# A two-layer decoder trunk: norm heads over six tiles, second statistics behind 18 products, a first FFN whose head weights have tiles of their own, and one more unit ahead of two waits of the scan

## The chip, the core and the metric

The kernel runs on one NeuronCore of a Trainium2 chip. The metric is the device time of one execution in microseconds; 0.3% of it is 3.6 us. The engines are PE (TensorE matmul; its weight loads are PEld), DVE (VectorE), ACT (ScalarE), POOL (GpSimd) and SP (SyncE, which here issues most of the DMAs).

## The reference, cut to what matters

The input is x (1 x 512 x 1024, fp32) and a conditioning vector c. There are two layers. Layer 0 mixes tokens with stick-breaking attention (16 heads), layer 1 with a diagonal complex state-space layer and a GLU; each is followed by a gated MLP with a causal convolution of width 3 (inner width 2816).

```python
def rms_norm(x, g):
    y = x * lax.rsqrt(jnp.mean(x * x, axis=-1, keepdims=True) + EPS)
    return y * g

for i in range(DEPTH):                       # DEPTH = 2
    mod = silu(c) @ w_mod[i] + b_mod[i]
    sh1, sc1, g1, sh2, sc2, g2 = jnp.split(mod, 6, axis=-1)
    h = rms_norm(x, norm_mix[i]) * (1 + sc1) + sh1
    y = stick_breaking_attention(h, ...) if i == 0 else s5_ssm(h, ...)
    x = x + g1 * y
    h = rms_norm(x, norm_ffn[i]) * (1 + sc2) + sh2
    x = x + g2 * conv_ffn(h, w_up[i], conv_w[i], conv_b[i], w_down[i])
return rms_norm(x, norm_out) * (1 + sc) + sh

def s5_ssm(h, ...):
    u = h @ w_in                             # then, in 64 groups of 16 channels,
    states = scan(lam_bar * state + b_bar @ u)
    y = real(c_mat @ states) + d_skip * u
    z = gelu(y)
    return (z * sigmoid(z @ w_glu + b_glu)) @ w_o
```

## The kernel before

**Layout and products.** Channels lie on the 128 partitions and the 512 tokens along the free axis, so x is eight tiles x0 to x7 of 128 x 512. Each fp32 matrix product is made of three products of a rounded high part and a rest: `mm3` (L155 on) issues hi by hi (L158), then weight-hi by input-lo (L161), then weight-lo by input-hi (L162). Such a triple over 512 columns is called a unit below. `load_w` (L143 on) brings a weight block of 0.5 MB into the ring `wraw` (three buffers, issued on SP, L150), ACT makes the high part (L152) and DVE the rest (L153), into rings `wH` and `wL` of `NW` = 5 buffers, or into tiles of the caller's own.

**Heads.** Three places have the same form: attention's output projection followed by the first FFN ("FFN0"), the first FFN's down projection followed by the state-space layer ("SSM"), and the SSM's output projection followed by the second FFN ("FFN1"). There `out_proj` (L339 on) finishes the last three tiles of x (x5, x6, x7) first for the left half of the tokens, then for the right (names ca and cb). ACT squares each updated tile (`acc_sq`, L226 and L229), DVE adds the squares into `acc` (L230), and `rstd_stat` (L263 on) sums `acc` over channels with a matmul of 1 column (L251, tile `stat`), takes the root on ACT (L255, tile `nsd`), refines it on DVE and writes a diagonal `dg`; `rstd_bc` (L270 on) broadcasts it with a matmul (L273, tile `rbc`). `sqrt_table` loads ACT's table for the root ahead of it (L241). Then `head_mm` runs: for the left half of the tokens, tile by tile, `norm_tile` writes hH and hL (DVE L291, ACT L298 and L300, DVE L304) and each of four weights is multiplied with it over 256 columns; the statistics and the broadcast of the right half stand among those products. It does so for the first `HEADK` = 5 tiles, then for the right half of the same tiles, and takes the remaining three over all 512 columns.

**The first FFN's first four weights.** Before, FFN0 loads them through the ring when `ffn` starts (`up_w`); FFN1's come by `head_w`, which `out_proj` calls after the weights of its own last three tiles and ahead of `sqrt_table`. `head_w` gives the first two of its four weights tiles of their own on the right side of the SBUF and leaves the other two to the ring. `HEADW` names the norm tiles behind which the next four weights are split.

**The scan.** After the SSM head, dense work (units of `u = h @ w_in`, later of the GLU) is cut into units that PE runs between the steps of the scan; `run(n)` issues n of them. Ahead of the loop stand `run(UPRE)`, step 0's `st_scan` (matmul `pv`, L1109), `run(USTG[0])`, step 1's, and `run(USTG[1])`. In each turn s of the loop, `st_out` issues `py` (L1109) and, on ACT, `yn` (L1178), `st_scan` issues `pv` for s, `run(1)` issues one unit, `st_tr` issues the transposes `pz` (L1183) that wait for `yn`, and `run(100)` the rest. On ACT the scan's states are written by L1165 (tile `st`, four instructions a step), and DVE runs the recurrence between (L1151 to L1160).

**What sets the order.** A scheduler that simulates the engines orders each engine's instructions, save those that are pinned to program order (`pinned`, `keep_in_program_order`), put behind another (`behind_head`, `follow`) or tied by data. Each engine then runs its own list in order.

Of the kernel before, what the change touches and what calls it, by code (L numbers as in the profile page):

```python
# [30 lines left out]
NW = 5  # L31
MIDK = 1
STATK = 0
HEADK = 5
HEADB = (3, 2)
HEADW = (4, 7, 10, 12)
UPRE = 10
NACC = 6
NIDLE = (7, 4, 4)
USTG = (7, 8)  # L40
BGU = 2
PACE = 12.0
NHOLD = 2
# [18 lines left out]
DUP = 's'  # L62
QK = 'kq'
BGA = 5
BGW = 0
ZM = ((1, 0), (1, 1), (3, 0), (3, 1))
OMB = 9
TAUX = 7
# [20 lines left out]
def _trunk(ctx, tc, I, out, tap):  # L89
# [105 lines left out]
    bgq = []  # L195
# [113 lines left out]
    def head_mm(R, h, a, b, hd):  # L309
        pin["head"] = []  # L310
        for cr in HALF + (FULL,):
            for k in range(HEADK) if cr != FULL else range(HEADK, KD):
                if cr.start == 0 and k == 2:
                    rstd_stat(R, HALF[1], True)
                norm_tile(h, k, R["bc"][0], a, b, cr)
                for q, (w, ps) in enumerate(hd):
                    if cr == HALF[0] and (k, q) == HEADB:
                        rstd_bc(R, HALF[1], None, True)
                    mm3(ps[:, cr], wk(w, k), (h[0][k][:, cr], h[1][k][:, cr]), k == 0 and cr.start == 0, k == KD - 1)
# [85 lines left out]
    def ffn(l, R, prep=None, last=None, hook=lambda: None):  # L405
# [4 lines left out]
        with ExitStack() as fc:  # L410
            fp = fc.enter_context(tc.tile_pool(name=f"ffn{l}", bufs=1, reuse_waits="tile"))

            def up_w(i, s):
                return load_w(up_src(l, i, s), name=f"up{l}_{i}_{s}"), bank(name=f"up{l}_{i}_{s}")


            todo = []
            i0 = 0
# [54 lines left out]
            for gi, gn in enumerate(GROUPS):  # L473
# [2 lines left out]
                if gi == 2:  # L476
                    hook()
                if gi == 0:
                    if l:
                        hx, ws = pin["hw"]  # L480
                        hd = [(q, s, ws[2 * q + s], bank(name=f"up{l}_{q}_{s}")) for q in range(2) for s in range(2)]
                    else:
                        hx = None
                        hd = [(q, s) + up_w(q, s) for q in range(2) for s in range(2)]
                    head_mm(R, h, a, b, [q[2:] for q in hd])
                    if hx:
                        hx.close()
                    for q in range(4):
                        with behind_head(pin["head"][HEADW[q]]):
                            split_next(False)  # L490
                    pin["prep"] = [pin["split"]]
                    for q in range(2):
                        gs.append(unit_out(q, q, [hd[2 * q + s][3] for s in range(2)]))
                    i = 2
                    step = prep(fc) if prep else (lambda: None)
# [31 lines left out]
    def attention(acc, late):  # L527
        with ExitStack() as ac:
# [282 lines left out]
            split(6)  # L811
            window(8, wo_units(range(KPRE, 7)))
            split(7)
            acc2 = new_acc()
            R = out_proj(wsrc, list(zip(oh, ol)), mcol(0, 2, 0), acc2, "wo", part=[(w, ps, 7) for w, ps in part], after=lambda: bg(BGW))
            bg(max(0, len([q for q in bgq if q[0] is not None]) - 72 - 8))
        return R


# [248 lines left out]
    def ssm(R):  # L1068
# [3 lines left out]
        with ExitStack() as zc:  # L1072
# [3 lines left out]
            with ExitStack() as sc:  # L1076
# [147 lines left out]
                for s_ in range(2, 10):  # L1224
                    st_out(s_ - 2)
                    if s_ < 8:
                        st_scan(s_)
                        load_out(s_)
                    if s_ + 1 < 8:
                        load_scan(s_ + 1)  # L1230
                    if s_ > 2:
                        if s_ == 3:
                            zh = new_h()
                            gb = [bank(name=f"glu{mt}") for mt in range(NGLU)]
                        glu_units(s_ - 3)
                    run(1)
                    st_tr(s_ - 2)
                    if s_ >= 8:
                        with behind_head([pin["comb"]]):
                            bg(11 - s_, False)  # L1240
                    run(100)
# [214 lines left out]
```

## Time and profile before

| What | Value |
|---|---|
| time before, median of three runs | 1212.62 us (1210.58 to 1214.79) |
| profiled execution, its own time | 1211.41 us |
| its span, first to last instruction | 1209.4 us |
| mean granted TensorE clock | 0.989 |
| PE busy | 1173.0 us, 97% |
| DVE, ACT, POOL busy | 884.2, 563.8, 264.0 us |

The profiled execution lies 1.21 us below the median of the three runs. Of its time, 2.0 us lie outside the span of instructions. In the span the FFN0 head stands at about 255 to 307 us, FFN0 itself to about 640, the SSM head to about 680, the scan to 790, and the FFN1 head at 832 to 868. In the timeline views a row has a start, a duration, the engine, the line and what it wrote and read; the brackets at its end hold the idle time of that engine just before it, and what ended that.

### The profile page before, as it was taken

The page shows a single profiled execution, that of the slowest core. Times are in us where ns is not written, and L with a number is a line of the kernel's source. Part 1 is how long each engine was busy: PE and PEld are TensorE (multiplying, and loading weights), DVE is VectorE, ACT ScalarE, POOL GpSimd, SP SyncE. Part 2 cuts the span into 40 slices and gives each one's busy share as a digit, 9 for nine tenths or more (in the row PEclk, how much of TensorE's full clock was granted, in tenths as well). Part 3 has the DMA queues.
Part 4 walks back from the last instruction along what each step waited for, and adds up shares of the span by engine and source line. Part 5 has one row for each costly group of instructions (what it writes and reads, how often), then busy time and mean ns, then how long its engine had stood idle before and what let it go on. Part 6 is the DMA issues. An engine that isn't in the chain of part 4 may idle for free.

```text
span 1209.4 us, 16352 instructions
## 1 busy us (share of the span) xinstructions
PE 1173.0 (97%) x6182; PEld 962.7 (80%) x6182; DVE 884.2 (73%) x1298; ACT 563.8 (47%) x886; POOL 264.0 (22%) x241
## 2 busy tenths in 40 slices
PE   8999999899999999989999999999999999999997
PEld 6877776588788787868888878789888888888887
DVE  6968888756896399997886679776598457744655
ACT  6756566346553133422444657744554234422443
POOL 1000000000098699989630000000000000000003
PEclk9999999899999999989999999999999999999999
DMA  8875555421234867878665599542257438532221
GB/s 306 319 242 174 192 175 190 157 88 53 73 119 131 239 235 225 252 229 291 217 184 152 188 292 342 186 159 68 70 175 236 130 106 208 157 110 82 79 79 70
DMA packets 93536, 210.99 MB, mean 174 GB/s; under 512 B 19601, under 2 KB 39953, under 8 KB 93458
## 3 DMA queue, kind: packets, MB, share of 16 engines
q1 hardware_dynamic: 85138, 207.86, 54.1%
q10 hardware_dynamic: 8320, 2.10, 0.8%
q8 instruction: 48, 0.79, 0.3%
q14 instruction: 30, 0.25, 0.1%
HBM read 188.68 MB, written 21.24 MB: 174 GB/s over the span
## 4 chain that ended last, share of the span: by engine, by line
PE 66%; DVE 12%; POOL 8%; DMA 6%; ACT 4%; issue 3%; SPq 2%; POOLq 0%; ACTq 0%; DVEq 0%
PE up L161 9%; PE up L162 9%; PE up L158 9%; PE dn L161 5%; PE dn L158 5%; PE dn L162 5%; PE o L756 1%; DMA bt<-in_b_imT_dram 1%; PE wo L158 1%; PE wos L158 1%; DVE ca L443 1%; PE wos L162 1%; PE wos L161 1%; PE wo L162 1%; PE wo L161 1%
## 5 line engine op out<-in xcount | busy, mean ns | idle before, releaser
L162 PE MATMUL up<-hH,up_l 128*128 128x512 f32 (+1 forms) x692 | 265.0, 385 | 4.9 <-DVE up_l L153 4.9
L161 PE MATMUL up<-hL,up_h 128*128 128x512 f32 (+1 forms) x692 | 264.9, 385 | 0.3 <-DVE hL L304 0.2
L158 PE MATMUL up<-hH,up_h 128*128 128x512 f32 (+1 forms) x692 | 261.3, 385 | 1.1 <-ACT hH L298 1.1
L443 DVE SCALAR_TENSOR_TENSOR ca<-up,small,ca 128x511 f32<-128x511 f32 (+1 forms) x176 | 131.4, 747 | 85.4 <-ACT ca L441 82.5
L183 DVE SCALAR_TENSOR_TENSOR wg<-wg,cact 128x1024 f32<-128x1024 f32 x96 | 125.1, 1318 | 42.4 <-DMA wg<-in_w_modT_dram 42.2
L162 PEld LDWEIGHTS up<-hH,up_l 128*128 128x128 f32 x692 | 130.5, 189 | 32.1 <-DVE up_l L153 6.8
L161 PEld LDWEIGHTS up<-hL,up_h 128*128 128x128 f32 x692 | 130.4, 189 | 26.4 <-DVE hL L304 0.9
L158 PEld LDWEIGHTS up<-hH,up_h 128*128 128x128 f32 x692 | 128.3, 188 | 27.9 <-ACT hH L298 1.5
L161 PE MATMUL dn<-gL,dn_h 128*128 128x512 f32 (+1 forms) x394 | 145.5, 369 | 2.7 <-DVE gL L458 2.7
L158 PE MATMUL dn<-gH,dn_h 128*128 128x512 f32 (+1 forms) x394 | 145.7, 371 | 0.5 <-ACT gH L457 0.5
L162 PE MATMUL dn<-gH,dn_l 128*128 128x512 f32 (+1 forms) x394 | 145.3, 369 | 0.0
L152 ACT ACTIVATE up_h<-up_r 128x1024 fp32r<-128x1024 f32 x84 | 88.3, 1053 | 107.6 <-DMA up_r<-in_w_up_dram 54.0
L153 DVE TENSOR_TENSOR up_l<-up_r,up_h 128x1024 fp32r<-128x1024 f32 x84 | 124.5, 1482 | 15.8 <-ACT up_h L152 14.9
L1328 POOL TENSOR_SCALAR xa<-x,Anorm_out 128x256 f32<-128x256 f32 x7 | 5.8, 828 | 576.3 <-ACT dn_h L152 561.5
L441 ACT ACTIVATE ca<-up,small 128x512 f32<-128x512 f32 x88 | 67.8, 771 | 102.4 <-PE up L162 102.4
L161 PEld LDWEIGHTS dn<-gL,dn_h 128*128 128x128 f32 x394 | 74.9, 190 | 15.3 <-DVE gL L458 3.0
L158 PEld LDWEIGHTS dn<-gH,dn_h 128*128 128x128 f32 x394 | 74.8, 190 | 13.7 <-ACT gH L457 0.9
L162 PEld LDWEIGHTS dn<-gH,dn_l 128*128 128x128 f32 x394 | 74.9, 190 | 12.2
L334 DVE SCALAR_TENSOR_TENSOR x<-dn,mod,x 128x512 f32<-128x512 f32 (+1 forms) x55 | 37.3, 679 | 61.1 <-PE dn L162 61.0
L450 ACT ACTIVATE ca<-ca 128x512 f32<-128x512 f32 x44 | 27.8, 633 | 90.1 <-DVE ca L443 88.4
L152 ACT ACTIVATE dn_h<-dn_r 128x1024 fp32r<-128x1024 f32 (+1 forms) x48 | 46.6, 981 | 49.8 <-PE dn L161 36.6
L153 DVE TENSOR_TENSOR dn_l<-dn_r,dn_h 128x1024 fp32r<-128x1024 f32 (+1 forms) x48 | 63.7, 1328 | 3.2 <-ACT dn_h L152 3.0
(304 smaller groups left out, 2258.8 us busy)
## 6 DMA issues: line engine op xcount, KB each, us to landing
wg<-in_w_modT_dram SPq DMA_DIRECT2D x96, 512.0 KB
up_r<-in_w_up_dram SPq DMA_DIRECT2D x84, 512.0 KB
dn_r<-in_w_down_dram SPq DMA_DIRECT2D x32, 512.0 KB
wgs<-in_w_modT_dram SPq DMA_DIRECT2D x16, 512.0 KB
dn_r<-in_w_down_dram SPq DMA_DIRECT2D x16, 384.0 KB
wv_r<-in_w_v_dram SPq DMA_DIRECT2D x8, 512.0 KB
wk_r<-in_w_qk_dram SPq DMA_DIRECT2D x8, 512.0 KB
wq_r<-in_w_qk_dram SPq DMA_DIRECT2D x8, 512.0 KB
```

The source lines that it names most:

```text
L152: order("S", lambda: S.activation(wh[:, :n], raw[:, :n], AF.Copy))
L153: pin["split"] = order("V", lambda: V.tensor_tensor(wl[:, :n], raw[:, :n], wh[:, :n].bitcast(F32), ALU.subtract))
L158: ins = PE.matmul(ps, ah, bh, start=start, stop=False)
L161: PE.matmul(ps, ah, bl, start=False, stop=False)
L162: PE.matmul(ps, al, bh, start=False, stop=stop)
L183: mul = lambda: V.scalar_tensor_tensor(w, w, 1.0, cact, ALU.mult, ALU.mult, accum_out=raw[:, col:col + 1])
L334: add = lambda: V.scalar_tensor_tensor(xs, pv, gate, xs, ALU.mult, ALU.add)
L441: follow("S", lambda: S.activation(ca, ps, AF.Identity, bias=small[:, cb:cb + 1], scale=tapw[2]))
L443: follow("V", lambda: V.scalar_tensor_tensor(ca[:, q:], ps[:, :T - q], tapw[2 - q], ca[:, q:], ALU.mult, ALU.add))
L450: follow("S", lambda: S.activation(cg, cg, AF.Silu))
L756: ins = PE.matmul(po[pr][h2 * HD:(h2 + 1) * HD, j * P:], vn[:, j, hd:hd + HD], src, start=j == 0, stop=j == 3)
L1328: G.tensor_scalar(xa[k], x[k][:, cb], a[:, k:k + 1], 0.0, ALU.mult, ALU.add)
```

## The change

It has four parts. (Behind the first FFN's code the lines of the kernel now are eight lower: L1109 is L1101, L1178 is L1170, L1183 is L1175.) `HEADK` goes from 5 to 6 in all three heads, and the second `rstd_stat` moves in the code from ahead of norm tile 2 (24 matmuls in) to inside tile 1 behind its second weight (18 matmuls in). FFN0's first four weights come by `head_w` under the name `upo`, as FFN1's do, and so are loaded inside attention's `out_proj`, which is now called after attention's own pool is closed; the two remaining calls of `bg` there are dropped (they ran no step, as 58 of at most 80 were left). `HEADW` counts norm tiles and follows `HEADK`, so that its weights are split behind the same tiles as before or one later. In the scan, `UPRE` goes from 10 to 12, `USTG` from (7, 8) to (6, 7), and the loop's `run(1)` becomes `run(2)`.

```diff
--- before.py
+++ after.py
@@ -31,13 +31,14 @@
 NW = 5
 MIDK = 1
 STATK = 0
-HEADK = 5
+HEADK = 6
+HEADS = (1, 2)
 HEADB = (3, 2)
-HEADW = (4, 7, 10, 12)
-UPRE = 10
+HEADW = (4, 8, 11, 13)
+UPRE = 12
 NACC = 6
 NIDLE = (7, 4, 4)
-USTG = (7, 8)
+USTG = (6, 7)
 BGU = 2
 PACE = 12.0
 NHOLD = 2
@@ -62,7 +63,6 @@
 DUP = 's'
 QK = 'kq'
 BGA = 5
-BGW = 0
 ZM = ((1, 0), (1, 1), (3, 0), (3, 1))
 OMB = 9
 TAUX = 7
@@ -310,10 +310,10 @@
         pin["head"] = []
         for cr in HALF + (FULL,):
             for k in range(HEADK) if cr != FULL else range(HEADK, KD):
-                if cr.start == 0 and k == 2:
-                    rstd_stat(R, HALF[1], True)
                 norm_tile(h, k, R["bc"][0], a, b, cr)
                 for q, (w, ps) in enumerate(hd):
+                    if cr == HALF[0] and (k, q) == HEADS:
+                        rstd_stat(R, HALF[1], True)
                     if cr == HALF[0] and (k, q) == HEADB:
                         rstd_bc(R, HALF[1], None, True)
                     mm3(ps[:, cr], wk(w, k), (h[0][k][:, cr], h[1][k][:, cr]), k == 0 and cr.start == 0, k == KD - 1)
@@ -410,9 +410,6 @@
         with ExitStack() as fc:
             fp = fc.enter_context(tc.tile_pool(name=f"ffn{l}", bufs=1, reuse_waits="tile"))
 
-            def up_w(i, s):
-                return load_w(up_src(l, i, s), name=f"up{l}_{i}_{s}"), bank(name=f"up{l}_{i}_{s}")
-
 
             todo = []
             i0 = 0
@@ -476,15 +473,10 @@
                 if gi == 2:
                     hook()
                 if gi == 0:
-                    if l:
-                        hx, ws = pin["hw"]
-                        hd = [(q, s, ws[2 * q + s], bank(name=f"up{l}_{q}_{s}")) for q in range(2) for s in range(2)]
-                    else:
-                        hx = None
-                        hd = [(q, s) + up_w(q, s) for q in range(2) for s in range(2)]
+                    hx, ws = pin["hw"]
+                    hd = [(q, s, ws[2 * q + s], bank(name=f"up{l}_{q}_{s}")) for q in range(2) for s in range(2)]
                     head_mm(R, h, a, b, [q[2:] for q in hd])
-                    if hx:
-                        hx.close()
+                    hx.close()
                     for q in range(4):
                         with behind_head(pin["head"][HEADW[q]]):
                             split_next(False)
@@ -811,9 +803,9 @@
             split(6)
             window(8, wo_units(range(KPRE, 7)))
             split(7)
-            acc2 = new_acc()
-            R = out_proj(wsrc, list(zip(oh, ol)), mcol(0, 2, 0), acc2, "wo", part=[(w, ps, 7) for w, ps in part], after=lambda: bg(BGW))
-            bg(max(0, len([q for q in bgq if q[0] is not None]) - 72 - 8))
+        acc2 = new_acc()
+        R = out_proj(wsrc, list(zip(oh, ol)), mcol(0, 2, 0), acc2, "wo", part=[(w, ps, 7) for w, ps in part],
+                     head=([up_src(0, q, s) for q in range(2) for s in range(2)], "upo"))
         return R
 
 
@@ -1233,7 +1225,7 @@
                             zh = new_h()
                             gb = [bank(name=f"glu{mt}") for mt in range(NGLU)]
                         glu_units(s_ - 3)
-                    run(1)
+                    run(2)
                     st_tr(s_ - 2)
                     if s_ >= 8:
                         with behind_head([pin["comb"]]):
```

**FFN0's head on ACT.** The rows stand behind the split of the last weight of attention's projection, `wo7`; `up0_i_s` and `upo0` to `upo3` are the FFN's first four weights, `sq` is a square of a tile of x (x5 to x7 by halves). Before:

```order
L241 ACT_TABLE_LOAD
L241 ACTIVATE warm_2364<-ones_102 128x1
L229 ACTIVATE sq_2263<-x1_79 128x512
L229 ACTIVATE sq_2270<-x2_80 128x512
L152 ACTIVATE up0_0_0_h_2576<-up0_0_0_r_2575 128x1024
L229 ACTIVATE sq_2305<-x3_81 128x512
L152 ACTIVATE up0_0_1_h_2583<-up0_0_1_r_2582 128x1024
L229 ACTIVATE sq_2340<-x4_82 128x512
L229 ACTIVATE sq_2393<-x5_83 128x256
L229 ACTIVATE sq_2421<-x6_84 128x256
L229 ACTIVATE sq_2449<-x7_85 128x256
L152 ACTIVATE up0_1_0_h_2590<-up0_1_0_r_2589 128x1024
```

And now:

```order
L229 ACTIVATE sq_2264<-x1_79 128x512
L229 ACTIVATE sq_2271<-x2_80 128x512
L152 ACTIVATE upo0_h_2369<-upo0_r_2368 128x1024
L229 ACTIVATE sq_2306<-x3_81 128x512
L152 ACTIVATE upo1_h_2375<-upo1_r_2374 128x1024
L152 ACTIVATE upo2_h_2381<-upo2_r_2380 128x1024
L229 ACTIVATE sq_2341<-x4_82 128x512
L152 ACTIVATE upo3_h_2387<-upo3_r_2386 128x1024
L241 ACT_TABLE_LOAD
L241 ACTIVATE warm_2392<-ones_102 128x1
L229 ACTIVATE sq_2421<-x5_83 128x256
L229 ACTIVATE sq_2449<-x6_84 128x256
```

The table load and its warm-up have moved from ahead of the first square to behind the split of the fourth weight, and the splits of the third and fourth weight from behind the left half's squares of x5 to x7 to ahead of them.

**FFN0's head on PE.** `stat` are the second statistics; around them stand the four weights' products with hH and hL (L158, L161, L162 over 256 columns). Before:

```order
L158 MATMUL up_1_0_2595<-hH_2557,up_1_0_h 128x256
L158 MATMUL up_1_1_2602<-hH_2557,up_1_1_h 128x256
L251 MATMUL stat<-ones,acc 128x1 x2
L161 MATMUL up_0_0_2581<-hL_2565,up_0_0_h 128x256
L162 MATMUL up_0_0_2581<-hH_2557,up_0_0_l 128x256
```

And now:

```order
L158 MATMUL up_1_0_2604<-hH_2584,upo_h 128x256
L158 MATMUL up_1_1_2605<-hH_2584,upo_h 128x256
L251 MATMUL stat<-ones,acc 128x1 x2
L161 MATMUL up_0_0_2602<-hL_2592,upo_h 128x256
L162 MATMUL up_0_0_2602<-hH_2584,upo_l 128x256
```

The second statistics stand in the same place of PE's list as before, behind the high products of the third norm tile; the broadcast that follows 20 products later (tile `rbc`) is in its old place too. It is the same in FFN1's head; in the SSM head the statistics stand four products earlier and the broadcast in its old place.

**The scan on PE, turn 2, step 0's transposes.** `u` is the dense work; `pv` is step 2's, `pz` step 0's. Before:

```order
L1109 MATMUL py_6525<-pC,st_6322 64x128 x8
L1109 MATMUL pv_6545<-u,pB 64x64 x16
L158 MATMUL u_6494<-hH_5992,win_h 128x512
L161 MATMUL u_6494<-hL_6000,win_h 128x512
L162 MATMUL u_6494<-hH_5992,win_l 128x512
L1183 MATMUL pz<-consts,yn 128x128 x4
L158 MATMUL u_6494<-hH_5993,win_h 128x512
L161 MATMUL u_6494<-hL_6001,win_h 128x512
```

And now:

```order
L1101 MATMUL py_6565<-pC,st_6362 64x128 x8
L1101 MATMUL pv_6585<-u,pB 64x64 x16
L158 MATMUL u_6537<-hH_6014,win_h 128x512
L161 MATMUL u_6537<-hL_6022,win_h 128x512
L162 MATMUL u_6537<-hH_6014,win_l 128x512
L158 MATMUL u_6537<-hH_6015,win_h 128x512
L161 MATMUL u_6537<-hL_6023,win_h 128x512
L162 MATMUL u_6537<-hH_6015,win_l 128x512
L1175 MATMUL pz<-consts,yn 128x128 x4
L158 MATMUL u_6537<-hH_6016,win_h 128x512
```

A second unit of three products stands between `pv` and `pz`. It is so in each turn.

**The scan on ACT, the same turn.** `st` are the states of a step, `wglk_h` a split of a GLU weight, `z` reads the transposes. Before:

```order
L1115 ACTIVATE ut<-u_6424 128x512
L1116 DMA sU<-ut 128x8x64
L1165 ACTIVATE st_6323<-m_6478 64x4x63 x4
L152 ACTIVATE wglk_h<-wglk_r 128x640
L1178 ACTIVATE yn<-py_6525 128x4x8x16
L1186 ACT_TABLE_LOAD
L1186 ACTIVATE z_6010<-pz 64x4x64 x4
```

And now:

```order
L1107 ACTIVATE ut<-u_6470 128x512
L1108 DMA sU<-ut 128x8x64
L1170 ACTIVATE yn<-py_6565 128x4x8x16
L1157 ACTIVATE st_6363<-m_6521 64x4x63 x2
L152 ACTIVATE wglk_h<-wglk_r 128x640
L1157 ACTIVATE st_6363<-m_6521 64x4x63 x2
L1178 ACT_TABLE_LOAD
L1178 ACTIVATE z_6032<-pz 64x4x64 x4
```

`yn` of step 0 has moved from behind the four `st` of step 1 and a weight split to ahead of them.

## The prediction

> **What bounds the kernel now.** I read the page's busy times first, then its chain.
>
> ```profile
> PE 1173.0 (97%) x6182; PEld 962.7 (80%) x6182; DVE 884.2 (73%) x1298; ACT 563.8 (47%) x886; POOL 264.0 (22%) x241
> PE 66%; DVE 12%; POOL 8%; DMA 6%; ACT 4%; issue 3%; SPq 2%; POOLq 0%; ACTq 0%; DVEq 0%
> ```
>
> PE works 97% of the span, so the change can win only where PE idles or is throttled. Then I cut the span into stages and asked what PE waited for in each (columns: PE, PEld, DVE, ACT, POOL busy, granted clock, DMA share, GB/s; for a wait: total us, times, longest).
>
> ```profile
> 255.00:286.00 31.00, 28.94 (x222) 27.67 (x221) 24.83 (x52) 19.35 (x32) 0.00 (x0) 1.00 0.40 120
> 305.00:326.00 21.00, 20.88 (x93) 16.95 (x91) 19.28 (x66) 10.54 (x15) 0.00 (x0) 1.00 0.22 75
> 442.00:523.00 81.00, 76.45 (x371) 60.81 (x369) 79.81 (x69) 33.77 (x47) 78.51 (x50) 1.00 0.79 241
> 705.00:790.00 85.00, 82.22 (x750) 67.56 (x748) 70.12 (x118) 61.72 (x118) 0.00 (x0) 1.00 0.80 270
> PE stat L251 <- DVE acc L230: 0.9, 1, 0.9
> PE up L162 <- DVE up_l L153: 4.9, 4, 2.2
> PE dn L161 <- DVE gL L458: 2.7, 1, 2.7
> PE pz L1183 <- ACT yn L1178: 2.8, 4, 1.2
> ```
>
> The FFN0 head (255 to 286) loses 2.1 us and the scan (705 to 790) 2.8. In FFN0 itself PE waits 4.9 for splits and 2.7 for gL, while DVE (79.81 of 81 us) and POOL are full.
>
> **The change part by part.** *Six tiles by halves.* These PE rows (and one of DVE) give the spacing of products and the head's main stall:
>
> ```profile
> 269.70 0.28 PE L161 MATMUL wo<-hL,wo_h 128*128 128x256 f32 x1
> 269.82 0.28 PE L162 MATMUL wo<-hH,wo_l 128*128 128x256 f32 x1
> 271.00 0.61 PE L251 MATMUL stat<-ones,acc 128*128 128x1 f32 x4 [0.91 <-DVE acc L230]
> 283.93 0.59 PE L273 MATMUL rbc<-dg,ones 128*128 128x256 f32 x2
> 285.67 0.74 PE L158 MATMUL up<-hH,up_h 128*128 128x256 f32 x4 [1.15 <-ACT hH L298]
> 325.26 0.39 PE L158 MATMUL up<-hH,up_h 128*128 128x512 f32 x1
> 325.49 0.39 PE L161 MATMUL up<-hL,up_h 128*128 128x512 f32 x1
> 325.49 1.22 DVE L153 TENSOR_TENSOR up_l<-up_r,up_h 128x1024 fp32r<-128x1024 f32 x1
> 326.76 0.50 PE L162 MATMUL up<-hH,up_l 128*128 128x512 f32 x1 [0.89 <-DVE up_l L153]
> ```
>
> A 256-column product takes 0.12 us (269.70 to 269.82), a 512-column one 0.23 (325.26 to 325.49; 0.227 over longer runs). Twelve wide ones become 24 narrow ones in each head: 24 x 0.12 - 12 x 0.227 = +0.16 us, three times +0.47. Behind the second broadcast, PE waits for the first right-half hH (1.15 us). The sixth left tile could cover that only if its products stood behind the broadcast. They do not: statistics and broadcast stand behind the third and fourth tile in the FFN heads as before, and what follows waits for hH of the next tile. I price this part's gain at zero; the cover that would be needed, 12 narrow products, is 1.44 us, which bounds the gain at 1.15 in each head. Moving the SSM's statistics four products up has no wait in the trace to remove: zero.
>
> *FFN0's own weight tiles.* ACT's list in the head, and DVE's last step before the statistics:
>
> ```profile
> 258.50 1.28 ACT L241 ACT_TABLE_LOAD   x1
> 259.79 0.20 ACT L241 ACTIVATE warm<-ones 128x1 f32<-128x1 f32 x1
> 261.44 1.06 ACT L152 ACTIVATE up_h<-up_r 128x1024 fp32r<-128x1024 f32 x1 [0.40 <-DMA up_r<-in_w_up_dram]
> 264.02 1.06 ACT L152 ACTIVATE up_h<-up_r 128x1024 fp32r<-128x1024 f32 x1 [0.72 <-DMA up_r<-in_w_up_dram]
> 268.38 0.95 ACT L229 ACTIVATE sq<-x 128x256 f32<-128x256 f32 x2 [0.92 <-DVE acc L230]
> 270.98 0.40 ACT L229 ACTIVATE sq<-x 128x256 f32<-128x256 f32 x1
> 270.54 0.41 DVE L230 TENSOR_TENSOR acc<-acc,sq 128x256 f32<-128x256 f32 x1
> 264.19 0.33 SPq L150 DMA_DIRECT2D up_r<-in_w_up_dram  x1
> ```
>
> Now the left squares of x5 to x7 stand behind the split of the fourth weight and the table load. The first two weights reached ACT at 261.44 and 264.02, 2.58 apart; the fourth, issued at 264.19 when the ring's first buffer came free, can then be split at about 261.44 + 3 x 2.58 = 269.2. From there: split 1.06, table 1.28, warm 0.20 and three squares (0.95 + 0.40) end at 269.2 + 3.9 = 273.1, one accumulation (0.41) at 273.5, and with 0.15 for hand-overs (my choice) the statistics start at 273.65, against 271.00: +2.65 us. This counts the transfers as one after another. If the fourth took only 2.58 from its issue, it would land at 266.8, and ACT, held by the third split and the square of x4 then, would come some 1.5 us sooner: +1.1, the lower bound.
>
> PE would then stand still from 269.94 to 273.65, 3.7 us. The next rows tell what a stall does to the clock:
>
> ```profile
> 416.82 0.61 PE L162 MATMUL up<-hH,up_l 128*128 128x512 f32 x1 [2.22 <-DVE up_l L153]
> 523.38 0.80 PE L161 MATMUL dn<-gL,dn_h 128*128 128x512 f32 x1 [2.67 <-DVE gL L458]
> 417.10:420.50 3.40, 3.40 (x9) 2.61 (x9) 1.38 (x2) 0.09 (x1) 2.23 (x3) 0.50 1.03 370
> 523.00:529.80 6.80, 6.42 (x28) 4.49 (x29) 6.80 (x7) 1.06 (x1) 4.11 (x3) 0.51 0.89 271
> ```
>
> After the wait of 2.22 the granted clock is 0.50 for 3.4 us, after that of 2.67 for 6.8; at half clock half of that time is lost, so a stall of 3.7 costs a further 1.7 (one window) to 3.4 (two); I take one. [...]
>
> On the other side, two splits (DVE L153, 1.2 us each) that stood behind the head now come inside it. That takes 2.4 us from DVE in the stage 305 to 326, where it is 92% busy and at whose end PE waits 0.89. By spacing that wait costs 326.76 - 325.49 - 0.227 = 1.04; a bracket counts some 0.15 less than is lost, and I add that to the others. This wait goes: -1.04. FFN0 so comes to 327 by 0.16 + 2.65 + 1.7 - 1.04 = 3.47 us late. What later waits return of this depends on whether their releasers come from PE. The largest, at 416.82, does not:
>
> ```profile
> SPq L955 <- POOL tb L835: 16.0, 1, 16.0
> POOL tt L834 <- ACT si L888: 86.4, 1, 86.4
> ```
>
> SP's transfers, the split's among them, were held by a store that waited 16.0 us for POOL, and POOL's work began behind ACT's `si`, whose preparation on DVE stands beside FFN0's own steps and gains the 2.4 us. So if PE comes 3.47 later, the wait there (2.22 + 0.15) and the loss in the throttled window behind it (3.4 x 0.5 = 1.7), together 4.1, can go. A whole return has the 2.4 us for it, none the order of DVE's list; I take three quarters, -3.0. FFN0 in all: +0.47.
>
> *The scan.* Its waits by place:
>
> ```profile
> 698.72 1.15 PE L1109 MATMUL pv<-u,pB 128*64 128x64 f32 x32 [0.84 <-issue]
> 716.54 0.66 PE L1183 MATMUL pz<-consts,yn 128*128 128x128 f32 x4 [1.20 <-ACT yn L1178]
> 746.49 0.66 PE L1183 MATMUL pz<-consts,yn 128*128 128x128 f32 x4 [0.24 <-ACT yn L1178]
> 760.79 0.66 PE L1183 MATMUL pz<-consts,yn 128*128 128x128 f32 x4 [1.10 <-ACT yn L1178]
> 715.27 0.74 ACT L152 ACTIVATE wglk_h<-wglk_r 128x640 fp32r<-128x640 f32 x1
> 715.91 0.58 ACT L1178 ACTIVATE yn<-py 128x512 f32<-128x512 f32 x1
> 726.00:733.00 7.00, 6.76 (x83) 5.51 (x82) 6.62 (x13) 5.08 (x12) 0.00 (x0) 1.00 1.04 368
> ```
>
> A unit is 3 x 0.227 = 0.68 us. The first `pv` waited 0.84 + 0.15 for u's way through DRAM; two units ahead of it, 1.36, cover that: -1.0. The `pz` at 716.54 waited 1.35: a unit takes 0.68, and `yn` now runs ahead of the split at 715.27 (0.74): -1.35. The one at 746.49 waited 0.39, and so did the fourth of the group (2.8 less 1.2, 1.1 and 0.24): -0.8. The last, 1.25, keeps what a unit leaves: -0.68. The sum is -3.8. Between the steps each `pv` needs operands from DRAM, and the DMA share is full (1.04 at 726), so part may come back: I take -3.5, with bounds of -0.5 (transfers hold each step where it was, and half of the first wait's gain is left) and -3.8.
>
> *The rest* (the dropped `bg` calls, the pool's end) issues nothing: zero.
>
> **The sum.** Heads of SSM and FFN1 +0.31, FFN0 +0.47, scan -3.5: -2.7. The profiled execution's 1211.41 becomes 1208.7; it lies 1.21 below the median of the runs, 1212.62, which becomes **1209.9 us**. About 0.3%, 3.6 us, is what a measurement of this kernel can tell from no change; this is less.
>
> **The rivals.** (A, the forecast) as summed: 0.37. A fifth of it goes beyond -3.6: with the scan's whole 3.8 and the whole 4.1 at 416.82 it is -4.1.
>
> (B) The later waits return nothing, because DVE's preparation stands behind FFN0's delayed steps in its list: 3.0 more than A, +0.3: 1212.9. For it speaks that DVE is full from 442 to 523; against it, the 2.4 us it gains. 0.17.
>
> (C, the other side) The statistics' stall throttles the head for three windows: 10.2 us at half clock cost 5.1 instead of 1.7, none of it returns, and the split at 326.76 is late all the same. Then 0.47 + 2.65 + 5.1 - 3.5 = +4.7: 1217.3. It decides once the clock stays at 0.5 for more than two windows of 3.4 us: the granted clock from 274 to 284 would read 0.5, as the head's next wait (285.67) comes before PE is steady. For it speaks that the 2.67 already cost two windows; against it, that the 2.22 cost one. 0.14.
>
> (D) The transfers keep the scan's pace: -0.5 there, +0.3 in all: 1212.9. The share of 1.04 speaks for it; against it, that `pz` waits for ACT in all four cases. 0.06.
>
> (E) The fourth weight lands early, FFN0 loses 1.1 and no window, and the 2.4 us that DVE gains reach the wait at 416.82: 0.16 + 1.1 - 1.04 - 2.4 = -2.2, with the scan and 0.31 -5.4: 1207.2, and 1205.5 if the throttled window goes too. For it: three transfers are under way at once. 0.17.
>
> (F) The change does in the heads what the rows of PE's list deny: the sixth tile's products cover the broadcast, and three waits of 1.15 go beside A, -3.45: 1206.5. 0.06.
>
> (G) ACT stays held behind the moved table load for another 1.28, the load's own length: 1.3 more than A, 1211.2. The row at 259.79 speaks against it. 0.03.
>
> **Chances and range.** Faster by over 0.3%: a fifth of A, E, F: 0.07 + 0.17 + 0.06 = 0.30. Slower: C, 0.14. Within: 0.56. The range reaches from E's lower end, 1205.5, to 1217.3, the time of C; outside lie half of C and the tails of E and F, some 0.12. A's own range, by the bounds of its terms, is 1208.5 to 1212.9.
>
> **What would show it.** In the head the statistics near 273.6 with a wait on `acc` of about 3.5 and a clock of 0.5 behind them; no wait at 326, a shorter one near 417. In the scan no wait of `pz` before the last and none at the first `pv`. The 1.15 behind each second broadcast still there. The forecast is wrong if the statistics stand before 272, if the wait near 417 keeps its 2.2, or if the stage to 790 is not 3 us shorter.

## The result, and the profile after

The changed kernel takes 1216.07 us (median of 20 runs, 1210.98 to 1221.14); the kernel before, over 20 runs beside them, 1211.88 (1207.1 to 1215.73). The ratio is 1.0031 (95% interval 1.0019 to 1.0043): 3.8 us slower, where 2.7 us faster was forecast.

The profiled execution of the changed kernel is a slow one among its runs (1219.35 us, span 1217.2), so its whole is not compared with 1209.4. The two traces are set side by side by stage, from the first narrow product of attention's last three tiles on. Columns: what the stage runs from and to, before, after, difference.

| Stage | before | after | |
|---|---|---|---|
| start to the first narrow `wo` product | 258.4 | 261.3 | +2.9 |
| FFN0's head and FFN0, to the first product of the SSM | 405.8 | 410.0 | +4.2 |
| SSM head and scan, to the first `wos` product | 125.5 | 126.0 | +0.5 |
| SSM's projection | 45.4 | 45.4 | 0.0 |
| FFN1's head and FFN1, to PE's last product | 367.6 | 367.8 | +0.2 |

The first row lies ahead of every changed instruction but the issue of the first weights, 0.6 us before its end. In the 14 kernels profiled here that stretch takes between 258.4 and 265.0 us, also in kernels that have the same instructions there, so it says nothing of the change. The second row scatters as well: two kernels of the experiments that differ from the kernel before only in the scan take 403.3 and 403.2 us there, where it took 405.8. So its +4.2 may be wrong by 2.6.

PE's waits of the changed kernel in FFN0's head, in FFN0 and in the SSM (total us, times, longest):

```profile
PE stat L251 <- DVE acc L230: 4.6, 1, 4.6
PE up L162 <- DVE up_l L153: 5.3, 7, 1.1
PE dn L161 <- DVE gL L455: 2.7, 1, 2.7
PE pv L1101 <- DMA pB<-sB: 3.0, 1, 3.0
PE pz L1175 <- ACT yn L1170: 1.2, 2, 0.7
336.19 0.50 PE L162 MATMUL up<-hH,up_l 128*128 128x512 f32 x1 [0.68 <-DVE up_l L153]
```

The wait at the statistics has grown from 0.9 to 4.6. The split waits in FFN0 sum to 5.3 where they were 4.9, but the longest has fallen from 2.2 to 1.1. The one at 326, which was to go, is still there (the last row, 0.68 instead of 0.89). In the scan the waits for `yn` have fallen from 2.8 to 1.2, as forecast, and the first `pv` no longer waits; in their place stands one wait of 3.0 that was not there before. ACT's list in FFN0's head and the statistics on PE, as forecast in kind:

```profile
264.24 1.06 ACT L152 ACTIVATE upo_h<-upo_r 128x1024 fp32r<-128x1024 f32 x1 [1.80 <-DMA upo_r<-in_w_up_dram]
266.72 1.06 ACT L152 ACTIVATE upo_h<-upo_r 128x1024 fp32r<-128x1024 f32 x1 [0.50 <-DMA upo_r<-in_w_up_dram]
269.63 1.06 ACT L152 ACTIVATE upo_h<-upo_r 128x1024 fp32r<-128x1024 f32 x1 [1.86 <-DMA upo_r<-in_w_up_dram]
273.15 1.06 ACT L152 ACTIVATE upo_h<-upo_r 128x1024 fp32r<-128x1024 f32 x1 [1.94 <-DMA upo_r<-in_w_up_dram]
274.23 1.28 ACT L241 ACT_TABLE_LOAD   x1
275.63 0.70 ACT L229 ACTIVATE sq<-x 128x256 f32<-128x256 f32 x2
277.60 1.01 PE L251 MATMUL stat<-ones,acc 128*128 128x1 f32 x4 [4.59 <-DVE acc L230]
```

ACT waits 1.94 for the fourth weight, splits it, loads the table and only then squares the left halves; the statistics start 4.45 us behind the start of the fourth split. The clock in the stretch behind (columns as in the prediction), beside the SSM's two windows around the new wait:

```profile
272.70:277.60 4.90, 0.31 (x3) 0.11 (x2) 3.20 (x7) 3.99 (x7) 0.00 (x0) 0.92 0.51 159
277.60:283.60 6.00, 6.00 (x28) 6.00 (x29) 1.53 (x8) 0.26 (x1) 0.00 (x0) 0.50 0.13 53
740.00:747.00 7.00, 7.00 (x85) 5.95 (x84) 6.60 (x13) 5.38 (x13) 0.00 (x0) 1.00 0.43 129
747.00:754.00 7.00, 4.05 (x69) 3.33 (x67) 4.03 (x7) 4.74 (x10) 0.00 (x0) 1.00 0.97 330
```

The half clock lasts two windows of 3.4 us, from 276.8, while PE still waits, to 283.6. In the scan the DMA share falls to 0.43 ahead of the wait: it is not that the loads were too slow, they were not issued. SP and ACT's queue there:

```profile
729.30 0.39 ACTq L1108 DMA_DIRECT2D sU<-ut  x1
735.89 1.37 SPq L1082 DMA_DIRECT2D pT<-sT  x1
744.85 0.32 SPq L1083 DMA_DIRECT2D pC<-sC  x1
SPq L1083 <- DMA sU<-ut: 7.5, 1, 7.5
752.96 1.15 PE L1101 MATMUL pv<-u,pB 128*64 128x64 f32 x32 [2.95 <-DMA pB<-sB]
```

SP stands from 737.3 to 744.85 ahead of a load of `pC`, for the landing of the last store of `u`, which ACT issued at 729.30. So that store took 15.5 us; the `pB` behind `pC` in SP's list came too late for `pv`. Why `pC` waits for a store that it does not read stands in the instructions' own waits (order of the changed kernel):

```
ACT  L1108 DMA sU_116<-ut_6658 128x8x64 [waits DMAHW5_49,Activation_49]
SP   L1083 DMA pC_6836<-sC_111 128x1024 [waits DMAHW5_49,PE_49]
```

Both name the semaphore `DMAHW5_49`, and `pC` is the next DMA on it behind the store. Its wait for the landing is the 7.5 us above.

### The profile page after: what moved, and what is told of

It reads as the page before. It is cut to its first block, busy times and chain, and to the rows that moved or that the text cites. A ratio compares the mean times of both kernels' runs of the same rounds, so it can differ in the third digit from the quotient of the medians.

```text
span 1217.2 us, 16434 instructions
## 1 busy us (share of the span) xinstructions
PE 1175.4 (97%) x6218; PEld 966.4 (79%) x6218; DVE 884.6 (73%) x1304; ACT 563.8 (46%) x892; POOL 264.0 (22%) x241
## 4 chain that ended last, share of the span: by engine, by line
PE 72%; DVE 12%; DMA 6%; ACT 4%; issue 3%; POOL 2%; SPq 1%; POOLq 0%; ACTq 0%; DVEq 0%
PE up L158 10%; PE up L161 10%; PE up L162 10%; PE dn L158 6%; PE dn L161 6%; PE dn L162 6%; DVE om L718 2%; DVE up_l L153 2%; DVE ca L440 1%; DMA up_r<-in_w_up_dram 1%; PE wos L158 1%; PE wos L162 1%; PE wos L161 1%; DVE wg L183 1%; PE u L161 1%
## 5 line engine op out<-in xcount | busy, mean ns | idle before, releaser
L162 PE MATMUL up<-hH,up_l 128*128 128x512 f32 x640 | 249.6, 391 | 5.3 <-DVE up_l L153 5.3
L158 PE MATMUL up<-hH,up_h 128*128 128x512 f32 x640 | 250.2, 391 | 0.5 <-ACT hH L298 0.5
L161 PE MATMUL up<-hL,up_h 128*128 128x512 f32 x640 | 249.3, 389 | 0.0
L161 PE MATMUL dn<-gL,dn_h 128*128 128x512 f32 (+1 forms) x394 | 144.8, 368 | 2.7 <-DVE gL L455 2.7
L162 PEld LDWEIGHTS up<-hH,up_l 128*128 128x128 f32 x640 | 120.1, 188 | 33.2 <-DVE up_l L153 8.5
L158 PE MATMUL dn<-gH,dn_h 128*128 128x512 f32 (+1 forms) x394 | 145.4, 370 | 0.0
L162 PE MATMUL dn<-gH,dn_l 128*128 128x512 f32 (+1 forms) x394 | 144.5, 367 | 0.0
L158 PEld LDWEIGHTS up<-hH,up_h 128*128 128x128 f32 x640 | 120.1, 188 | 26.7 <-issue 1.0
L161 PEld LDWEIGHTS up<-hL,up_h 128*128 128x128 f32 x640 | 120.2, 188 | 24.6
L152 ACT ACTIVATE up_h<-up_r 128x1024 fp32r<-128x1024 f32 x80 | 84.1, 1052 | 101.8 <-PE dn L161 37.8
L153 DVE TENSOR_TENSOR up_l<-up_r,up_h 128x1024 fp32r<-128x1024 f32 x80 | 118.3, 1479 | 11.8 <-ACT up_h L152 10.9
L161 PEld LDWEIGHTS dn<-gL,dn_h 128*128 128x128 f32 x394 | 74.6, 189 | 15.1 <-DVE gL L455 3.0
L158 PEld LDWEIGHTS dn<-gH,dn_h 128*128 128x128 f32 x394 | 74.4, 189 | 12.9 <-issue 0.6
L162 PEld LDWEIGHTS dn<-gH,dn_l 128*128 128x128 f32 x394 | 74.6, 189 | 12.3
```

The lines of the kernel that those rows point to most:

```text
L152: order("S", lambda: S.activation(wh[:, :n], raw[:, :n], AF.Copy))
L153: pin["split"] = order("V", lambda: V.tensor_tensor(wl[:, :n], raw[:, :n], wh[:, :n].bitcast(F32), ALU.subtract))
L158: ins = PE.matmul(ps, ah, bh, start=start, stop=False)
L161: PE.matmul(ps, ah, bl, start=False, stop=False)
L162: PE.matmul(ps, al, bh, start=False, stop=stop)
```

## The experiments

All ratios are to the kernel before, run beside them on the same chip, over five rounds.

**Each part alone.** Theory T1 held FFN0's own weight tiles for the loss, T2 the six tiles by halves, T3 the stretch ahead. The first kernel is the kernel before with FFN0's head weights by `head_w`:

```diff
-            R = out_proj(wsrc, ..., after=lambda: bg(BGW))
+        R = out_proj(wsrc, ...,
+                     head=([up_src(0, q, s) for q in range(2) for s in range(2)], "upo"))
```

> The kernel before with one part of the change alone: the first FFN's four head weights by head_w (own tiles, loaded inside attention's out_proj). Theory T1 (the loss of the whole change, +0.31%, is this part: ACT's list in the first FFN's head holds the left squares behind the fourth split and the table load): statistics there wait over 4 us, the granted clock is 0.5 for two windows behind them, the head loses 6 us, later waits give back 2; in all +4 us, ratio 1.0033. Theory T2 (the loss comes from six tiles by halves in all three heads): ratio 1.000, no such wait. Theory T3 (the loss lies in attention, where the changed kernel's trace is 2.9 us later by 212 us, from where tiles lie): +2.9 before 212 us again.

1217.01 us, ratio 1.0050 (1.0032 to 1.0068). T1's wait and clock are there:

```profile
278.39 0.92 PE L250 MATMUL stat<-ones,acc 128*128 128x1 f32 x4 [3.72 <-DVE acc L229]
278.52:285.35 6.83, 6.83 (x32) 6.83 (x33) 1.88 (x9) 0.35 (x2) 0.00 (x0) 0.50 0.10 38
```

The wait is 3.72 and the half clock lasts 6.83 us. By the medians this part alone loses more than the whole change, but the intervals (1.0032 to 1.0068 and 1.0019 to 1.0043) overlap.

The scan's counts alone:

```diff
-UPRE = 10
+UPRE = 12
-USTG = (7, 8)
+USTG = (6, 7)
-                    run(1)
+                    run(2)
```

> The kernel before with the scan's counts alone (UPRE 12, USTG (6, 7), run(2)). Theory S1 (the waits for yn and u go, -3.2 us, and come back as one wait of pv for its operand, about 3 us, since SP stands behind the landing of the last store of u): the wait of pv, 3 us, is there at about 742 us, the waits of pz are down to 1.5 in all; net -0.5 to +0.5 us, ratio 1.000. Theory S2 (that wait comes only with the later phase that the slower head gives): no such wait, -3 us, ratio 0.9975.

1210.37 us, ratio 0.9989 (0.9974 to 1.0004): no clear difference. Waits in the scan, SP's and PE's:

```profile
SPq L1091 <- DMA sU<-ut: 6.2, 1, 6.2
745.54 1.15 PE L1109 MATMUL pv<-u,pB 128*64 128x64 f32 x32 [1.11 <-DMA pB<-sB]
```

SP's wait is there without the slow head, so S2 falls; but it costs PE 1.1 in this execution, not 3. SSM head and scan take 123.7 us here against 125.5 before, 1.9 less.

The heads alone (`HEADK`, `HEADS`, `HEADW`, as in the diff of the change):

> The kernel before with the heads alone (HEADK 6, HEADS, HEADW). T1: +0.5 us (36 more narrow products), ratio 1.0004, three waits of 1.15 behind the second broadcasts as before. T2: +4 us, ratio 1.003.

1212.22 us, ratio 1.0002 (0.9988 to 1.0017): T2 falls. And the change without its own tiles, that is, heads and scan together:

> The changed kernel with the first FFN's head weights back in the ring, as before (heads and scan as changed). T1: the statistics in the first FFN's head wait 0.9 again and no clock window follows; time of the kernel before, ratio 0.999 to 1.001. T2: ratio 1.003. T3: ratio 1.0007 with attention as before.

1210.01 us, ratio 0.9988 (0.9972 to 1.0004). The statistics and the clock behind them:

```profile
277.33 0.61 PE L252 MATMUL stat<-ones,acc 128*128 128x1 f32 x4 [0.91 <-DVE acc L231]
277.33:292.00 14.67, 13.52 (x109) 13.07 (x109) 10.37 (x31) 7.50 (x17) 0.00 (x0) 1.00 0.21 73
```

The wait is 0.91 again and the clock holds. With the own tiles the same kernel had 1.0031: by division they cost 0.43% (0.23 to 0.63), about 5 us. T1 stands. T3 falls too: this kernel's trace has 264.8 us ahead of the first narrow product, the changed kernel's 261.3, and it is the faster one.

**What in the own tiles costs.** The changed kernel with the table load ahead of the head weights:

```diff
+        if head and nm == "wo":
+            sqrt_table()
         if head:
             pin["hw"] = head_w(*head)
-        sqrt_table()
+        if not (head and nm == "wo"):
+            sqrt_table()
```

> The changed kernel with the table load and its warm-up back ahead of the head weights' splits (the fourth split still ahead of the left squares). Theory T1a (the statistics wait for a chain: fourth weight's landing, split, table load, squares): the table's 1.28 and the warm-up leave the chain, the wait falls by about 1.4 us, from 4.6 to 3.2; the clock still drops behind it, for one or two windows; ratio 1.001 to 1.002. Theory T1b (the table load alone is the cause): the wait falls to 1 and the clock holds; ratio 0.998.

1213.89 us, ratio 1.0023 (1.0008 to 1.0038).

```profile
279.43 0.61 PE L251 MATMUL stat<-ones,acc 128*128 128x1 f32 x4 [2.80 <-DVE acc L230]
280.95:284.35 3.40, 3.40 (x19) 3.40 (x18) 0.68 (x4) 0.00 (x0) 0.00 (x0) 0.50 0.05 19
275.27 1.06 ACT L152 ACTIVATE upo_h<-upo_r 128x1024 fp32r<-128x1024 f32 x1 [0.95 <-DMA upo_r<-in_w_up_dram]
276.36 1.23 DVE L153 TENSOR_TENSOR upo_l<-upo_r,upo_h 128x1024 fp32r<-128x1024 f32 x1 [0.31 <-ACT upo_h L152]
277.90 1.85 DVE L230 TENSOR_TENSOR acc<-acc,sq 128x256 f32<-128x256 f32 x4
```

The wait falls to 2.80, and one window of half clock follows: T1b falls. But little of the fall is the table load's. From the start of the fourth split (275.27) to the statistics it takes 4.16 us, against 4.45. The rest comes from the fourth weight, whose split starts 10.3 us behind the first narrow product in this execution and started 11.8 us behind it in the changed kernel's. The chain has a second branch, on DVE, nearly as long as the one over the table load: the fourth weight's residual (276.36) stands ahead of the sums of the left squares (277.90). So T1a's number came out in part by luck.

Then the fourth split, and with it its residual, goes behind the left squares as well; the call of `head_w` moves behind the left halves of `out_proj` for that:

```diff
+        with tc.issue_after(pin["sq"].ins) if late else ExitStack():
             order("S", lambda: S.activation(wh[:, :n], raw[:, :n], AF.Copy))
```

> The changed kernel with the table load first and the fourth weight's split behind the left squares (own tiles, heads and scan as changed). T1a: the statistics no longer wait for the fourth weight; DVE's residual of x5's right half stands ahead of the last accumulations, so about 2 us of wait are left (0.9 before); if that is short enough for the clock, the head's 6 us loss shrinks to 1 and the later waits' 2 us are gained: ratio 0.997 to 0.999. T1b: as table_first.

1211.02 us, ratio 0.9999 (0.9983 to 1.0014): 0.24% under the last one, the way that T1a said; the hoped 0.997 is not reached.

```profile
274.71 0.49 PE L252 MATMUL stat<-ones,acc 128*128 128x1 f32 x3 [1.96 <-DVE acc L231]
275.00:290.00 15.00, 13.86 (x111) 13.27 (x111) 9.46 (x31) 7.16 (x16) 0.00 (x0) 1.00 0.13 38
```

A wait of 1.96 leaves the clock at 1.00. From the last product ahead of the statistics to the last matmul of the second broadcast it takes 15.4 us, against 14.3 before, 17.7 with the table first, 20.6 in the changed kernel and 20.1 with own tiles alone.

To part wait and clock, 30 products that nothing reads fill the changed kernel's wait:

```diff
+                        for _ in range(30):
+                            pe_pin(PE.matmul(R["ps"][:, cb], wk(ws[0][1], 0)[0], rhs[0][0][:, ca], start=True, stop=True))
                     rstd_stat(R, ca, True)
```

> The changed kernel with 30 products of 256 columns added ahead of the first statistics of the first FFN's head; they write columns of the statistics' bank that nothing reads, and take 3.6 us of the 4.6 that PE waits there. Theory C1 (half of the head's loss is the clock: 0.5 for two windows, 3.4 us): the granted clock stays at 1.0, statistics and what follows stand as late as before, and the time falls by about 3 us, ratio 1.000 to 1.001. Theory C2 (at half clock PE only fills what it would wait for anyway): the clock stays at 1.0 but the time does not move, ratio 1.003.

1213.02 us, ratio 1.0017 (1.0003 to 1.0032).

```profile
271.82 3.76 PE L392 MATMUL stat<-hH,wo_h 128*128 128x256 f32 x30
275.42 0.50 PE L251 MATMUL stat<-ones,acc 128*128 128x1 f32 x4
275.00:290.00 15.00, 13.86 (x114) 13.40 (x113) 8.21 (x30) 6.25 (x14) 0.00 (x0) 1.00 0.06 25
```

The statistics are still late, the clock is held at 1.00, and from the last product ahead of the fill to the second broadcast it takes 16.7 us instead of 20.6. Of these 3.9 us the clock's part is 2.8; the other 1.1 come from the fourth weight, which lands earlier in this execution, so that the statistics start 3.7 us behind that product instead of 4.9. The ratio falls by 0.14%, between what C1 and C2 said; the intervals overlap, so the clock's share of the time is shown in the trace and only indicated in the ratio.

**The scan's new wait.** The counts alone, with the stores of `u` issued from POOL's queue:

```diff
-                    S.dma_start(sU[bi].rearrange("j p c -> p j c"), ut)
+                    G.dma_start(sU[bi].rearrange("j p c -> p j c"), ut)
```

> The kernel before with the scan's counts and the stores of u issued from POOL's queue instead of ACT's; the order on the other engines is as with the counts alone. Theory S1 (a pv waits because SP's queue stands behind the landing of the last store of u, which it meets as the DMA eight places ahead on the same semaphore): the store may still take over 10 us, but SP no longer waits for it, pv has no wait in turn 5, and the scan is 3 us shorter than before: ratio 0.9975. Theory S3 (the transfers themselves set the pace, the wait at the store is only where it shows): pv still waits 1 us or more and the ratio stays at 0.999.

1208.69 us, ratio 0.9984 (0.9971 to 0.9997). All that PE waits for between 680 and 790 us, and what is left of SP's wait:

```profile
PE pz L1183 <- ACT yn L1178: 1.5, 2, 1.0
SPq L1091 <- DMA u<-sU: 0.7, 1, 0.7
```

SP no longer waits for the store and `pv` no longer waits, so S1 holds for the place, and the wait of 1 us or more that S3 asked for is not there. The size is half of what was expected: 1.9 us by ratio, 2.4 in the trace (123.2 us for SSM head and scan), since `pz` still waits 1.5. In the six kernels with these counts and ACT's store, `pv` waited 3.0, 1.1, 0.5, 1.3 and twice not at all for its operand (SP behind the store for 7.5, 6.2, 6.2, 7.5, 4.5 and 4.0 us): it depends on how late the store lands in that execution. In the four with POOL's store it waited in none. That POOL's store gains time is not shown, however: SSM head and scan take 121.8 to 126.0 us in those six, 123.6 in the mean, and 123.2 in this kernel; with the old counts it is 125.2 to 125.5 in three kernels.

Both repairs on the changed kernel:

> Both repairs on the changed kernel: table load first, the fourth split behind the left squares, and the stores of u from POOL's queue. With T1a and S1: the head's loss is down to 1 us and the scan is 3 us shorter than before, ratio 0.995 to 0.997 to the kernel before. With T1b or S3: 0.998 or more.

1211.12 us, ratio 1.0008 (0.9995 to 1.0021): the 0.995 to 0.997 was not reached. Its trace has both waits mended (statistics 2.0, no `pv`); FFN0 behind the head takes 359.8 us, where the kernel with the fourth split behind, whose order there is the same, took 356.6. That scatter between executions hides what own tiles return in FFN0, so this stays open.

**The wait behind the second broadcast.** In DVE's list of the kernel before, the fifth left tile (x4) waits for PE and the right half's first tile (x0) does not (order, with waits):

```
L291 TENSOR_TENSOR nt1_2671<-x3_81,rbc_2525 128x256 [waits DVE_49]
...
L291 TENSOR_TENSOR nt1_2690<-x4_82,rbc_2525 128x256 [waits PE_49]
L291 TENSOR_TENSOR nt1_2708<-x0_78,rbc_2525 128x256
```

Both halves of the broadcast share one tile of PSUM, and the left tile that is issued behind the second broadcast waits for it, though it reads the other half (DVE's `nt` waits 1.3 us for `rbc` there). (No run puts the halves into two tiles, so whether that alone would part them is not shown.) The changed kernel keeps that order, with two left tiles behind it. The next kernel is the kernel before with the heads' part and the broadcast behind the fifth tile's products:

```diff
-HEADB = (3, 2)
+HEADB = (5, 0)
```

> The kernel before with the heads' part (six tiles by halves) and HEADB (5, 0) in place of (3, 2): the second broadcast is written behind the fifth tile's products. Theory H1 (the 1.15 us behind each second broadcast is a wait of the next left tile's nt for that broadcast, since both halves share one tile of PSUM; the sixth tile can cover it only if its nt is issued ahead of the broadcast): the wait of nt for rbc moves to the right half's first tile, 12 products (1.44 us) run under it, about 0.3 of the 1.15 is left in each head: -2.5 to -3 us, ratio 0.9975 to 0.998. Theory H2 (the left tile really needs the chain behind the second statistics): the wait stays or moves ahead of the broadcast, ratio 1.000.

1205.64 us, ratio 0.9954 (0.9936 to 0.9971), twice what was expected. FFN0's head on PE and the wait on DVE:

```profile
286.88 0.64 PE L159 MATMUL up<-hH,up_h 128*128 128x256 f32 x4
288.32 0.59 PE L274 MATMUL rbc<-dg,ones 128*128 128x256 f32 x2
288.56 0.83 PE L159 MATMUL up<-hH,up_h 128*128 128x256 f32 x4
288.95 0.75 DVE L292 TENSOR_TENSOR nt<-x,rbc 128x256 f32<-128x256 f32 x2 [0.91 <-PE rbc L274]
```

PE goes from the broadcast to the sixth tile with no wait; DVE's next `nt` waits for the broadcast while those 12 products run. The 1.15 is gone in all three heads, not reduced to 0.3: 1.40 each by spacing, 4.2 us. Shorter waits right behind it go too: the 28 products that follow each second broadcast take 3.76, 3.87 and 3.77 us, where they took 5.86, 5.96 and 5.84 in the kernel before. That is 6.3 us, less 0.47 for the narrow products 5.8; the ratio says 5.6 (3.5 to 7.8). H1 holds.

**Together.** Late broadcast, the scan's counts with POOL's stores, weights in the ring:

> Heads with the late broadcast, the scan's counts with the stores of u from POOL's queue, the first FFN's weights in the ring as before. The parts add if they are apart: scan -1.9 (scan_pool), heads -2.5: ratio 0.9955 to 0.9965. If the heads' gain is taken back by later waits: 0.998.

1205.97 us, ratio 0.9948 (0.9929 to 0.9966); the scan's part is not seen in the ratio beside the late broadcast alone, though the trace has 120.1 us for SSM head and scan against 122.9. And with own tiles, table first and fourth split behind:

> As mended, but with the first FFN's weights in tiles of their own, table load first and the fourth split behind the left squares. If own tiles are worth something once their wait is gone (the waits at 326 and 417 us shorter): 0.1 to 0.2% under mended. If they only cost the second microsecond of wait at the first statistics: 0.1% over it.

1203.87 us, ratio 0.9935 (0.9917 to 0.9953), the lowest median of all; the intervals of the last three overlap. Its statistics still wait 2.0 us (0.9 in the kernel ahead). All three beat the kernel before and the changed one.

## Why the prediction was wrong, point by point

Two steps failed, and one more was short. FFN0 was to give back 4.0 of what its head loses, and gave back nothing that the runs show. The scan was to gain 3.5, and a wait behind a store on another queue took most of that back. The clock was halved for two windows and not for one.

- **Heads, +0.47 and no gain.** Right: 1.0002, the three waits of 1.15 stand. But I named the wrong waiter. It is the fifth left tile, not the right half's first; the row that I had quoted did not say which half, and DVE's waits in the order do. Had I read them, I would have seen that six tiles can't cover anything while the broadcast stands where it does. Rival F gave such a cover 1.15 for each head; the traces gave 2.1, once the broadcast moved.
- **Statistics of FFN0, +2.65.** Right in kind, and right in size but for the profiled execution of the changed kernel. From the fourth split to the statistics I had 269.2 to 273.65, 4.45 us; the trace has 273.15 to 277.60, 4.45, though I had left out DVE's residual of the fourth weight, which is nearly as long as the branch that I added up. In that execution the landing is late: I took the weights 2.58 apart, and they came 2.48, 2.91 and 3.52 apart, and the wait grew by 3.7. Measured from the first narrow product I had the fourth split at 10.8 us; it starts at 11.8 in this trace, at 10.95 with own tiles alone (the wait is 3.72, the standstill that I forecast), and at 10.3 with the table first and with the fill. Why the landing scatters is open.
- **The clock, one window.** It was two; rows of both kinds had been quoted, and I took the smaller. Beyond the wait itself (3.7 more), the head lost another 2.6 of its 6.3, where I had 1.7. The waits of 3.72 and 4.59 cost two windows each, that of 2.80 with the table first one; the length alone does not decide (last section).
- **What FFN0 gives back, -4.0.** This is the step that failed most: no return is shown. The head lost 6.3 us, and 5.8 with own tiles alone; the runs lost about 5 (by division) and 6.1 (own tiles alone, 3.9 to 8.2). Of 6.3 + 0.16, 2.3 came back in the two traces compared (head and FFN0 +4.2), but that is within the scatter of 2.6. The wait at 326, taken off in full (-1.04), kept 0.68 of its 0.89. The wait at 417 fell to 1.3 by spacing and its throttled window went, but smaller waits of splits came up instead (seven instead of four, 5.3 in all). Nor does that wait go by the weights' tiles: it is 0.86 in the kernel with the late broadcast, POOL's stores and the ring, and 2.33 in the last one, with own tiles. The part at 417 was set by a choice, three quarters, with no row for it. (Rival G is out: the squares start at 275.63, 0.1 behind the end of the table load.)
- **The scan, -3.5.** The waits that were to go went (from 3.6 to 1.2 in sum). The step that failed is the one sentence on the DMA: I had transfers that are late because the queue is full, and gave that 0.06. The wait is SP's, 7.5 us behind a store on another queue, by a semaphore that both name; the order shows it, the profile of before has it as a wait of 0.2. It took 3.0 in the changed kernel's trace and less in others; over many runs the counts alone save about 1.3 us (-0.1%, not clear of zero), by the mean of the traces 1.8.
- **The sum.** Own tiles about +5 instead of +0.3, scan about -1.3 instead of -3.5, heads as forecast. Rival C came out at 1217.3, close to the 1216.07, with the right mechanism (statistics, clock, nothing returned). Its number is in part luck: its clock, with a third window that did not come, is 2.5 too much, and its scan gains 2.2 too much. The range held the time, the sign was wrong.

## What to carry to other kernels

Before moving loads ahead of a critical chain, list what each of them puts on every engine's queue, and price it by the latest landing and not by the mean spacing: here a split that waited 1.94 us for its weight stood ahead of squares that PE was waiting for (4.59), and its residual ahead of their sums. Do not book what later waits may give back without a row that shows what releases them. When an engine waits for a value that it should already have, look at the tile and not at the value: here the readers of two halves in one tile were tied together (PE waited 1.15 us behind each second broadcast), and the order in which they are issued decided who waits. A slow store on ACT's queue (15.5 us) held SP's queue here for 7.5 us, ahead of a load that does not read what it stored: look for the semaphore that both use.

## What of the hardware was not expected

Whether a wait halves the clock is not set by its length alone. PE rows of the kernel with the scan's counts alone, of the kernel with the table first, and of the last kernel, each with the clock of the stretch behind it:

```profile
421.11 0.50 PE L162 MATMUL up<-hH,up_l 128*128 128x512 f32 x1 [1.99 <-DVE up_l L153]
421.49:424.90 3.41, 3.41 (x10) 2.67 (x9) 2.14 (x4) 0.43 (x1) 3.00 (x3) 0.50 0.92 363
```

```profile
530.73 0.50 PE L161 MATMUL dn<-gL,dn_h 128*128 128x512 f32 x1 [2.48 <-DVE gL L458]
531.00:538.00 7.00, 7.00 (x45) 5.39 (x44) 7.00 (x7) 1.06 (x1) 6.78 (x6) 1.00 0.87 263
```

```profile
417.90 0.50 PE L163 MATMUL up<-hH,up_l 128*128 128x512 f32 x1 [2.33 <-DVE up_l L154]
418.00:425.00 7.00, 7.00 (x31) 5.80 (x32) 5.94 (x8) 2.52 (x3) 6.58 (x6) 1.00 0.92 330
```

A wait of 1.99 dropped it for 3.41 us, waits of 2.48 and 2.33 did not, nor did the 2.95 of `pv` (752.96) in the changed kernel. Ordered by length, with more waits of PE beside them:

| Wait of PE | Kernel | Granted clock behind it |
|---|---|---|
| 1.96, to 274.71 | fourth split behind | 1.00 |
| 1.99, to 421.11 | the scan's counts alone | 0.50 for 3.41 us |
| 2.22, to 416.82 | before | 0.50 for 3.4 us |
| 2.33, to 417.90 | the last kernel | 1.00 |
| 2.48, to 530.73 | table first | 1.00 |
| 2.48, to 524.20 | fourth split behind | 1.00 |
| 2.67, to 523.38 | before | 0.50 for 6.8 us |
| 2.73, to 532.21 | the changed kernel | 0.50 for 3.41 us |
| 2.80, to 279.43 | table first | 0.50 for 3.40 us |
| 2.95, to 752.96 | the changed kernel | 1.00 |
| 3.72, to 278.39 | own tiles alone | 0.50 for 6.83 us |
| 4.59, to 277.60 | the changed kernel | 0.50 for 6.83 us |

Of the eight between 2 and 3 us, four had a drop behind them and four had none. So a wait of that length had no fixed price here, and what decides is not shown: no run moved a wait and left its length. The drops of the changed kernel between 80 and 1200 us start at 82.23, 215.35, 276.79 and 532.79 us and last 3.41, 10.24, 6.83 and 3.41; the kernel before has one of 10.24 too, from 212.26.

The last store of `u` (0.25 MB) from ACT's queue took 7.5 to 10.5 us from issue to landing in the traces with one unit ahead of `pz` (7.9 in the kernel before), and 11.9 to 15.5 us with two (15.5 in the changed one), where six or seven loads of SP's queue were under way when it was issued instead of three to five. From POOL's queue it took 7.0 to 8.2, with five or six under way, so their number alone is not the reason, which stays open.
